# A written order for the feed-forward slots, other places for the first weight units, other engines and buffers for the output weights, and early homes in the Scan

## The chip, the cores and the metric

The kernel runs on one core of one Trainium2 chip. The metric is the device time of the whole program in microseconds (us). Of the kernel before there are three timed runs and one profiled execution, whose trace gives every time on the engines.

## The reference

The program is a trunk of two layers over 512 tokens of width 1024. Each layer is a feed-forward, a token mixer and a second feed-forward, each with a residual and a layer norm. The mixer is neighbourhood attention in the first layer and a bidirectional RWKV-7 scan in the second. The change touches the feed-forward and the end of the RWKV mixer:

```python
D_MODEL, SEQ, D_FF, DEPTH = 1024, 512, 2816, 2

def swiglu(x, w_in, w_out):
    gate, up = jnp.split(x @ w_in, 2, axis=-1)
    return (jax.nn.silu(gate) * up) @ w_out

def reference(x, ...):
    for i in range(DEPTH):
        x = layer_norm(DN_ALPHA * x + 0.5 * swiglu(x, ffn_w_in[i, 0], ffn_w_out[i, 0]), ln_g[i, 0], ln_b[i, 0])
        if i % 2 == 0:
            m = neighbourhood_attention(x, ...)
        else:
            m = rwkv7_bidir(x, ...)       # ends in ((y + bonus) * g) @ w_out
        x = layer_norm(DN_ALPHA * x + m, ln_g[i, 1], ln_b[i, 1])
        x = layer_norm(DN_ALPHA * x + 0.5 * swiglu(x, ffn_w_in[i, 1], ffn_w_out[i, 1]), ln_g[i, 2], ln_b[i, 2])
    return x
```

## The kernel before

**Precision.** Every float32 operand is held as a high and a low half (`split`, L276 to L280): ScalarE copies the raw tile to the high half (L279), VectorE subtracts it from the raw tile to get the low half (L280; another engine may be given for this second step). A product is three matmuls: high by high, high by low, low by high.

**The feed-forward** (`ffn`) runs four times. Its hidden width of 2816 is 22 column blocks f in 11 pairs c = 0 to 10. Pairs 0 to 2 (f = 0 to 5) are plain projections, whose weights `load_cols` brings into three tiles `w`. `gated` (L513) applies the silu (ScalarE, L516) and the product with the up half (VectorE, L517). From pair 3 on stands the written part, class `Seven`. There each pair is one slot: the even block is four plain products over half the depth (`plain`), the odd block is seven products of combined weights and combined tokens (`products`). The tokens' combinations are made ahead by `mixes`, parts 0 to 3. Each slot takes eleven weight units. A unit is a high and a low half in one of nine places: two halves of each of the three `w` tiles, two in `self.pair` and one in `self.one`, both ring tiles. `spots` gives out the places in turn, `weights` loads raws from memory into two raw tiles (four halves), combines them on VectorE and splits them into units.

In the written part the order of the engines' work is the order of the code. `slot` advances named generators by the words of FF_SEQ (L85): g is a piece of the plain block (the fifth g is its gated tile), s a step of the seven products, w a step of the weight generator, k a piece of the sums over the gated tile of the slot before, e the early output products of the slot before, u and z the sums over output weights (`Winograd.sums`: the first u asks for 1 MB of `w_out`, tile `ra`, L1126; the next ones make sums and splits of it; z is the third split of the pair before).

**The output part** (`Winograd`, `ffn_out`) multiplies the gated tiles by quarter blocks of `w_out`, again with combined quarters (V, t3, b22, t4). Its pieces go by c = 0, 2, 4, 6, 8, 10. The pieces c=0 and c=2 of V are opened inside the last slot, as extra steps of w (`opening`); the others by `load`, which picks the place of the raw piece and splits it. Every piece with c a multiple of four has its low half made on GpSimd, the rest on VectorE. `self.raws` is the pair of ring tiles xT that the feed-forward's input held until then.

**The Scan** (`outs`, L1932) begins the product with the RWKV output weights while the recurrence still runs. EARLY is 5: five row blocks of `w_out` are accumulated for each of eight half tiles n (four token tiles by two halves). Row blocks 0 and 1 have extra early homes, read for n = 0 and 1 (`soon`); the others are read from where they stay.

SyncE issues the DMAs of all this, in one order; ScalarE, VectorE and GpSimd each work in theirs.

Of the kernel before, what the change touches and what calls it, by code (L numbers as in the profile page):

```python
# [19 lines left out]
P = 128  # L20
D = 1024
S = 512
# [3 lines left out]
NT = S // P  # L26
# [51 lines left out]
EARLY = 5  # L78
# [3 lines left out]
DECAY = math.exp(-0.5)  # L82
GN_EPS = 64e-5
SEVEN = range(7, NF, 2)
FF_SEQ = ("g k w g w w k g w k z u g k w g s w s w s e e e s w s s u s s u s s u s e s w s e e w u")  # L85


A, B = slice(0, 64), slice(64, 128)
# [12 lines left out]
def flat2(ap):  # L101
    return ap[:, :D], ap[:, D:]


def flat(ap):
    return ap.rearrange("p a b -> p (a b)")


class Trunk:
# [28 lines left out]
    def home(self, pool):  # L138
        return self.ex or pool
# [324 lines left out]
    def ffn(self, xT, w_in, w_out, ln, nxt, lead=None):  # L464

        nc = self.nc
        npairs = NF // 2
        out = Winograd(self, w_out)
        seven = Seven(self, xT, w_in)
        with self.pool("fa") as pool:
            out.pool = pool
            keep = []
            posts = iter(())
            for c in range(npairs):
                if 2 * c + 1 in SEVEN:  # L480
                    with self.tc.manual_schedule(engines=MANUAL_SCAN):
                        raw = seven.slot(c, out, pool, posts)
                        posts = self.posts(c, raw, out, seven, keep, pool)
                        if c == npairs - 1:
                            list(posts)
                    continue
                with self.behind(*() if c or ln else (self.asked,)):
                    list(out.sums(c))
                raw = pool.tile([P, 8, 256], F32, name="ar", tag="ar", bufs=1)
                for j in range(2):  # L490
                    f = 2 * c + j
                    if f == 0:
                        pps = self.follow()
                    elif not pps:
                        us = self.units if f == 1 else [self.load_cols(w_in, FF * i + f * P, eng=nc.vector) for i in range(2)]
                        pps = [self.proj(u, pp, xT) for u, pp in zip(us, seven.banks(f))]
                    self.gated(pps.pop(0), pps.pop(0), raw[:, 3:7:3] if j else raw[:, 0:8:7])
                    if f < 4:
                        seven.mixes(f)
                    if c and j == 0:  # L500
                        list(out.early(c - 1))
                list(self.posts(c, raw, out, seven, keep, pool))
                if 2 * c + 3 in SEVEN:
                    seven.prepare()
            out.keep = {n: [k[:, n] for k in keep] for n in range(2)}
            late = npairs - 4
            out.raws = self.pair(F32)
            out.add("V", 0, out.b21, range(0, late))
            list(out.early(npairs - 1))
            out.add("V", 0, out.b21, range(late, npairs))  # L510
        return self.ffn_out(out, npairs, ln, nxt, lead)
# [403 lines left out]
class Seven:  # L915
# [57 lines left out]
    def slot(self, c, out, pool, posts):  # L973

        if 2 * c + 3 not in SEVEN:
# [3 lines left out]
                       w=self.work, k=posts, z=out.third(c - 1), u=out.sums(c, True))  # L979
        for name in FF_SEQ.split():  # L980
            next(threads[name], None)
# [12 lines left out]
    def spots(self):  # L994

        k = self.k
        two = lambda t: [h.rearrange("p (i f) -> p i f", i=2) for h in flat2(t)]
        tiles = [lambda: k.sb_w.tile([P, 2 * D], F32R, name="w", tag="w", bufs=k.nw) for _ in range(3)]
        spots = []
        for t in (tiles[0], tiles[1], lambda: self.pair, None, tiles[2]):  # L1000
            for s in two(t()) if t else [self.one]:
                spots.append(s)
                yield s
        while True:
            yield from spots

    def weights(self):
# [10 lines left out]
        def make(raw):  # L1018
            u = next(spots)
            k.split(u[:, 0], u[:, 1], raw)  # L1020
            self.units.append(u)
# [91 lines left out]
class Winograd:  # L1113
# [29 lines left out]
    def opening(self):  # L1143

        k = self.k
        raws = {}
        for c in (0, 2):
            raws[c] = k.raw()
            k.nc.sync.dma_start(raws[c].rearrange("p (c f) -> p c f", c=2), self.b21(c, 2))
            self.loads += 1  # L1150
            yield
        yield
        yield
        for c in (0, 2):
            u = k.sb_w.tile([P, 2 * D], F32R, name="w", tag="w", bufs=k.nw).rearrange("p (i f) -> p i f", i=2)
            k.split(u[:, 0], u[:, 1], raws[c])
            self.begun["b21", c] = u
            yield
# [56 lines left out]
    def load(self, src, c, lag):  # L1215
        k = self.k
        n = min(2, NF // 2 - c)
        if self.loads < 3:
            raw = k.raw()
        elif self.raws:  # L1220
            raw = self.raws[self.loads // 4 % 2][:, self.loads % 4 * D : self.loads % 4 * D + D]
        else:
            raw = self.pool.tile([P, D], F32, name="rw", tag="rw", bufs=4)
        self.loads += 1
        raw = raw[:, : n * 512]
        k.nc.sync.dma_start(raw.rearrange("p (c f) -> p c f", c=n), src(c, n))
        if lag or c == 2 and src != self.b21:
            u = self.pool.tile([P, 2, n * 512], F32R, name=f"wl{n}", tag=f"wl{n}", bufs=n)
        else:
            u = k.sb_w.tile([P, 2 * D], F32R, name="w", tag="w", bufs=k.nw)[:, : 2 * n * 512].rearrange("p (i f) -> p i f", i=2)  # L1230
        k.split(u[:, 0], u[:, 1], raw, k.nc.vector if c % 4 else k.nc.gpsimd)
        return u

    def begin(self, src):
# [153 lines left out]
class Scan:  # L1388
# [255 lines left out]
    def fetch(self, hp, z):  # L1644
        lw = self.lws[hp, z] = self.tile("lw", [P, NT, P], 2)
        self.nc.sync.dma_start(lw, self.dram["lw"][:, z, :, hp * P : (hp + 1) * P])
# [283 lines left out]
    def outs(self):  # L1930

        nc = self.nc  # L1932
        rows = lambda ap, k: ap[k * P : (k + 1) * P, :]
        home = lambda n: self.tile(n, [P, NC, 2, CH]).rearrange("p a b c -> p (a b c)")
        fetch = lambda ap, i: nc.sync.dma_start(ap, rows(self.w_out, i)).ins
        self.left = [rows(self.dram["x"], t) for t in range(NT)]
        soon = [home(n) for n in ("bk0", "ar0")]
        for i, ap in enumerate(soon):
            fetch(ap, i)
        yield  # L1940
        w = self.w = [self.az[2][:, i].rearrange("p a b -> p (a b)") for i in range(2)]
        w += [flat(self.wv)]
        fetch(w[2], 2)
        for i in range(EARLY - 1):
            nc.sync.dma_start(self.xv[:, i, :], self.dram["o"][:, i, :])
        yield
        w += [home(n) for n in ("bk1", "ar1")]
        w += [self.units[i][0].rearrange("p a b c d -> p (a b c d)") for i in (2, 4, 3)]
        for i in (3, 4, 0, 1):
            ask = fetch(w[i], i)  # L1950
        yield
        for n, (t, h) in enumerate((t, h) for t in range(NT) for h in range(2)):
            hs = slice(h * 512, (h + 1) * 512)
            x = self.tile(("e", "e2", "th")[n % 3], [P, S], 2)
            nc.sync.dma_start(x, rows(self.dram["x"], t)[:, hs])
            acc = self.k.bank("ag"[n % 2])
            for i in range(EARLY):
                u = soon[i] if n < 2 and i < 2 else w[i]
                self.wide(acc, self.xv[:, i, t * P : (t + 1) * P], u[:, hs], i == 0, i == EARLY - 1)
                if i < EARLY - 1:  # L1960
                    yield
            nc.vector.scalar_tensor_tensor(x, x, ALPHA, acc, ALU.mult, ALU.add)
            ask = nc.sync.dma_start(rows(self.dram["x"], t)[:, hs], x).ins
            if n == 0:
                with self.k.behind(ask):
                    for c in range(EARLY, ND - 1):
                        nc.sync.dma_start(w[c], rows(self.w_out, c))
            self.stored += 1
            self.reload()
            yield  # L1970
# [214 lines left out]
```

## Time and profile before

| What | us |
| --- | --- |
| timed runs, median of 3 | 2207.59 (2206.01 to 2210.19) |
| profiled execution, device time | 2204.11 |
| its span, first to last instruction | 2202.3 |
| median landing of a 256 KB raw half | 3.2 |
| median landing of the 1 MB `ra` | 8.1 |

The four feed-forwards lie in the span at about 20 to 375, 610 to 975, 975 to 1325 and 1840 to 2200 us; attention stands between the first two, the RWKV mixer between the third and the fourth. In the rows below, PE is the matmul engine, DVE is VectorE, ACT ScalarE, POOL GpSimd and SP SyncE. "PE bank L1200 <- ACT w L279" is a wait of PE at line 1200, ended by ScalarE's write of a tile `w` at line 279. Lines are those of the kernel before; in the changed kernel most lie one further on.

### The profile page before, as it was taken

The page shows a single profiled execution, that of the slowest core. Times are in us where ns is not written, and L with a number is a line of the kernel's source. Part 1 is how long each engine was busy: PE and PEld are TensorE (multiplying, and loading weights), DVE is VectorE, ACT ScalarE, POOL GpSimd, SP SyncE. Part 2 cuts the span into 40 slices and gives each one's busy share as a digit, 9 for nine tenths or more (in the row PEclk, how much of TensorE's full clock was granted, in tenths as well). Part 3 has the DMA queues.
Part 4 walks back from the last instruction along what each step waited for, and adds up shares of the span by engine and source line. Part 5 has one row for each costly group of instructions (what it writes and reads, how often), then busy time and mean ns, then how long its engine had stood idle before and what let it go on. Part 6 is the DMA issues. An engine that isn't in the chain of part 4 may idle for free.

```text
span 2202.3 us, 39167 instructions
## 1 busy us (share of the span) xinstructions
PE 2130.1 (97%) x15104; PEld 1724.3 (78%) x15104; DVE 1548.6 (70%) x2634; ACT 1087.3 (49%) x2119; POOL 513.4 (23%) x666
## 2 busy tenths in 40 slices
PE   9999989999999999899999999999999999999988
PEld 8798878888887888788888777535777558788866
DVE  7677766277486777587777669835898558677765
ACT  4354435367444454444455343636888444444434
POOL 1000025565300000340000053044788610000013
PEclk9999999999999999999999999999999999999999
DMA  6544493342243455924345754774444552544473
GB/s 190 180 158 153 154 359 121 105 126 82 96 138 130 155 171 174 361 104 155 134 155 168 263 207 144 257 240 123 119 137 130 175 188 74 167 156 163 156 282 139
DMA packets 180395, 368.39 MB, mean 167 GB/s; under 512 B 34320, under 2 KB 54416, under 8 KB 178160
## 3 DMA queue, kind: packets, MB, share of 16 engines
q1 hardware_dynamic: 180208, 365.89, 49.4%
q8 instruction: 118, 1.93, 0.4%
q14 instruction: 69, 0.57, 0.1%
HBM read 285.08 MB, written 68.68 MB: 161 GB/s over the span
## 4 chain that ended last, share of the span: by engine, by line
PE 69%; DVE 13%; DMA 11%; ACT 3%; issue 3%; POOL 0%; SPq 0%; ACTq 0%; DVEq 0%; POOLq 0%
PE bank L1200 14%; PE bank L1056 14%; PE bank L290 5%; PE bank L289 5%; PE bank L291 5%; DMA ra<-in_ffn_w_out_dram 5%; PE a L1393 5%; PE bank L352 4%; DMA raw<-in_ffn_w_out_dram 2%; DVE w L280 2%; DMA raw<-in_ffn_w_in_dram 2%; PE g L1719 2%; DVE ring L280 2%; DVE wx L280 1%; PE y L1393 1%
## 5 line engine op out<-in xcount | busy, mean ns | idle before, releaser
L280 POOL TENSOR_TENSOR w<-raw,w 128x1024 fp32r<-128x1024 f32 x34 | 83.5, 2461 | 1249.8 <-ACT w L279 1239.8
L279 ACT ACTIVATE w<-raw 128x512 fp32r<-128x512 f32 (+1 forms) x306 | 221.6, 732 | 252.9 <-DVE raw L1034 47.7
L1056 PE MATMUL bank<-xT,w 128*128 128x512 f32 (+1 forms) x1476 | 280.7, 344 | 4.5 <-ACT tmp L516 4.3
L1056 PEld LDWEIGHTS bank<-xT,w 128*128 128x128 f32 x1476 | 238.0, 189 | 43.0 <-ACT tmp L516 9.4
L280 DVE TENSOR_TENSOR w<-raw,w 128x512 fp32r<-128x512 f32 (+1 forms) x272 | 205.5, 765 | 64.0 <-ACT w L279 62.8
L1200 PE MATMUL bank<-w,ring 128*128 128x512 f32 x720 | 181.1, 409 | 29.2 <-ACT w L279 20.9
L1200 PE MATMUL bank<-wx,an 128*128 128x512 f32 x792 | 199.9, 392 | 0.0
L1200 PEld LDWEIGHTS bank<-w,ring 128*128 128x128 f32 x720 | 141.1, 198 | 66.5 <-ACT w L279 24.0
L1056 PE MATMUL bank<-xT,ring 128*128 128x512 f32 (+1 forms) x828 | 162.4, 350 | 11.6 <-ACT tmp L516 11.6
L1056 PEld LDWEIGHTS bank<-xT,ring 128*128 128x128 f32 x828 | 136.4, 190 | 34.8 <-ACT tmp L516 14.6
L1200 PEld LDWEIGHTS bank<-wx,an 128*128 128x128 f32 x792 | 142.9, 189 | 24.9
L279 ACT ACTIVATE ring<-raw 128x512 fp32r<-128x512 f32 (+1 forms) x147 | 103.5, 706 | 95.1 <-DVE raw L1034 19.1
L289 PE MATMUL bank<-xT,w 128*128 128x512 f32 x368 | 145.1, 394 | 2.5 <-DVE ar L517 2.5
L290 PE MATMUL bank<-xT,w 128*128 128x512 f32 x368 | 143.5, 390 | 0.0
L291 PE MATMUL bank<-xT,w 128*128 128x512 f32 x368 | 142.9, 390 | 0.0
L1056 PE MATMUL bank<-ring,w 128*128 128x256 f32 x1056 | 140.6, 283 | 0.0
L1056 PEld LDWEIGHTS bank<-ring,w 128*128 128x128 f32 x1056 | 135.5, 191 | 3.6
L1828 POOL TENSOR_TENSOR tm<-qs,zs 128x126 f32<-128x126 f32 (+22 forms) x248 | 107.8, 435 | 59.7 <-DVE qs L1821 22.1
L1830 POOL TENSOR_TENSOR zs<-zs,tm 128x126 f32<-128x126 f32 (+22 forms) x248 | 110.0, 444 | 19.5
L1129 DVE TENSOR_TENSOR ts<-ra 128x512 f32<-128x512 f32 x44 | 30.4, 690 | 112.5 <-DMA ra<-in_ffn_w_out_dram 101.3
L280 DVE TENSOR_TENSOR ring<-raw,ring 128x512 fp32r<-128x512 f32 (+1 forms) x123 | 85.7, 700 | 32.9 <-ACT ring L279 32.3
L280 DVE TENSOR_TENSOR wx<-ra,wx 128x512 fp32r<-128x512 f32 x132 | 89.0, 685 | 11.3 <-ACT wx L279 10.4
(383 smaller groups left out, 4600.6 us busy)
## 6 DMA issues: line engine op xcount, KB each, us to landing
raw<-in_ffn_w_in_dram SPq DMA_DIRECT2D x256, 256.0 KB, 3.2
ra<-in_ffn_w_out_dram SPq DMA_DIRECT2D x44, 1024.0 KB, 8.1
raw<-in_ffn_w_in_dram SPq DMA_DIRECT2D x48, 512.0 KB, 3.8
d_away<-away SPq DMA_DIRECT2D x44, 512.0 KB, 9.0
ring<-d_away SPq DMA_DIRECT2D x16, 1024.0 KB, 10.7
xT<-d_late SPq DMA_DIRECT2D x29, 512.0 KB, 9.6
xT<-in_ffn_w_out_dram SPq DMA_DIRECT2D x23, 512.0 KB, 9.4
d_late<-ts SPq DMA_DIRECT2D x44, 256.0 KB, 3.8
```

Source lines behind the costliest of these rows:

```text
L279: self.hi = self.nc.scalar.activation(h, raw, AF.Copy).ins
L280: self.lo = (eng or self.nc.vector).tensor_tensor(l, raw, h.bitcast(F32), ALU.subtract).ins
L289: nc.tensor.matmul(out, wh, xh, start=start, stop=False)
L290: nc.tensor.matmul(out, wh, xl, start=False, stop=False)
L291: nc.tensor.matmul(out, wl, xh, start=False, stop=stop)
L352: nc.tensor.matmul(acc[t, h], a, u[:, i, h * 512 : (h + 1) * 512], start=first and n == 0, stop=last and n == 2)
L1056: self.nc.tensor.matmul(out, w[:, i, cs], x(c)[j], start=start and c + n == 0, stop=stop and c == 3 and n == 2, skip_group_check=True)
L1200: self.nc.tensor.matmul(acc, lhs, u[:, i], start=bool(first) and m == 0, stop=last and m == 2, skip_group_check=more)
L1393: self.nc.tensor.matmul(out[hs], w[:, hs], x, start=start, stop=stop)
L1719: nc.tensor.matmul(pgs[h][:, j * P : (j + 1) * P], flat(bk[hs, q * 4 + j]), ar[hs, :, q * 4 + j], start=True, stop=True)
L1828: nc.gpsimd.tensor_tensor(tv, qs[:, s, 0:s].rearrange("p (a o) -> p a o", o=1).broadcast_to([P, s, n]), zs[:, s : s + 1, c0:].broadcast_to ...
L1830: nc.gpsimd.tensor_tensor(zs[:, 0:s, c0:], zs[:, 0:s, c0:], tv, ALU.add)
```

## The change

It has seven parts.

1. FF_SEQ is another order: "z u" moves to the slot's start, the fifth g (the gated tile of the plain block) ahead of the fifth w, and the early steps e ahead of a w.
2. The last part of the mixes is written after f = 4 rather than f = 3.
3. `spots` gives the two halves of `self.pair` and `self.one` first and the three `w` tiles after them.
4. `opening` asks for both raws in one step; the two splits come one step of w earlier.
5. `load` puts its third raw (c=4 of V) into the freed xT tile, not into one of the two raw buffers.
6. `load` makes all low halves on VectorE.
7. `outs` fetches row blocks 2 and 3 to early homes too, in halves, and reads `wv` fifth.

```diff
-FF_SEQ = ("g k w g w w k g w k z u g k w g s w s w s e e e s w s s u s s u s s u s e s w s e e w u")
+MIXED = (0, 1, 2, 4)
+FF_SEQ = ("g k z u w g w w k g w k g k g s w s w s e e e w s w s s u s s u s s u s e s w s e e w u")
...
-                    if f < 4:
-                        seven.mixes(f)
+                    if f in MIXED:
+                        seven.mixes(MIXED.index(f))
...
-        for t in (tiles[0], tiles[1], lambda: self.pair, None, tiles[2]):
+        for t in (lambda: self.pair, None, *tiles):
...
             raws[c] = k.raw()
             k.nc.sync.dma_start(raws[c].rearrange("p (c f) -> p c f", c=2), self.b21(c, 2))
             self.loads += 1
-            yield
+        yield
         yield
         yield
...
-        if self.loads < 3:
-            raw = k.raw()
-        elif self.raws:
+        if self.raws:
             raw = self.raws[self.loads // 4 % 2][:, self.loads % 4 * D : self.loads % 4 * D + D]
...
-        k.split(u[:, 0], u[:, 1], raw, k.nc.vector if c % 4 else k.nc.gpsimd)
+        k.split(u[:, 0], u[:, 1], raw)
...
-        soon = [home(n) for n in ("bk0", "ar0")]
-        for i, ap in enumerate(soon):
-            fetch(ap, i)
+        soon = {(2, h): self.tile(n, [P, S]) for h, n in enumerate(("k0", "r0"))}
+        soon.update({(3, h): flat(self.tile("lw", [P, NT, P], 2)) for h in range(2)})
+        for i, h in soon:
+            fetch(soon[i, h], i, part(h))
+        for i, n in enumerate(("bk0", "ar0")):
+            row = home(n)
+            fetch(row, i)
+            soon.update({(i, h): row[:, part(h)] for h in range(2)})
         yield
         w = self.w = [self.az[2][:, i].rearrange("p a b -> p (a b)") for i in range(2)]
+        w += [home(n) for n in ("bk1", "ar1")]
         w += [flat(self.wv)]
-        fetch(w[2], 2)
+        fetch(w[4], 4)
...
-        w += [home(n) for n in ("bk1", "ar1")]
         w += [self.units[i][0].rearrange("p a b c d -> p (a b c d)") for i in (2, 4, 3)]
-        for i in (3, 4, 0, 1):
+        for i in range(4):
             ask = fetch(w[i], i)
...
-                u = soon[i] if n < 2 and i < 2 else w[i]
-                self.wide(acc, self.xv[:, i, t * P : (t + 1) * P], u[:, hs], i == 0, i == EARLY - 1)
+                u = soon[i, n] if n < 2 and i < 4 else w[i][:, hs]
+                self.wide(acc, self.xv[:, i, t * P : (t + 1) * P], u, i == 0, i == EARLY - 1)
```

Where instructions move, the order of an engine shows it. First ScalarE (the engine of the high halves, line 279 before and 280 of the change) from the silu of the last slot of the first feed-forward into the output part. `raw` and `xT` tiles hold pieces of `w_out`, `w` their high halves. Before:

```order
L516 ACTIVATE tmp_2516<-bank_441 128x512
L1076 ACTIVATE bank_442<-bank_441 128x256
L1076 ACTIVATE tmp_2521<-bank_441 128x256
L1076 ACTIVATE tmp_2520<-bank_442 128x256
L1094 ACTIVATE tmp_2519<-bank_441 128x256
L1076 ACTIVATE tmp_2520<-bank_442 128x256
L279 ACTIVATE wx_2618<-ra_2496 128x512
L1104 ACTIVATE tmp_2519<-tmp_2520 128x256
L279 ACTIVATE w_2639<-raw_2514 128x1024
L279 ACTIVATE w_2649<-raw_2534 128x1024
L279 ACTIVATE wx_2652<-ra_2496 128x512
```

And the same place of ScalarE in the changed kernel:

```order
L517 ACTIVATE tmp_2514<-bank_441 128x512
L1077 ACTIVATE bank_442<-bank_441 128x256
L1077 ACTIVATE tmp_2519<-bank_441 128x256
L280 ACTIVATE w_2571<-raw_2532 128x1024
L1077 ACTIVATE tmp_2518<-bank_442 128x256
L1095 ACTIVATE tmp_2517<-bank_441 128x256
L1077 ACTIVATE tmp_2518<-bank_442 128x256
L280 ACTIVATE wx_2621<-ra_2458 128x512
L1105 ACTIVATE tmp_2517<-tmp_2518 128x256
L280 ACTIVATE w_2642<-raw_2534 128x1024
L280 ACTIVATE wx_2652<-ra_2458 128x512
L280 ACTIVATE w_2701<-xT_2672 128x1024
```

The piece c=0 (`w_2639`, now `w_2571`) is split five instructions earlier, in the middle of the products; c=4 (now `w_2701`, out of a part of an xT tile) follows right behind c=2 and ahead of the last `wx`, where before seven instructions stood between.

Second VectorE at the entry of the first slot of the first feed-forward. `ar` is the tile of the gated blocks, `ring_767` its kept part, `raw_774` and `raw_775` the weight generator's raw tiles, `w_780`, `w_787` and `w_818` tiles of units, `ring_260` is `self.pair` and `ring_261` `self.one`. Before:

```order
L517 SCALAR_TENSOR_TENSOR ar_619<-bank_442,tmp_678 128x2x256
L280 TENSOR_TENSOR w_780<-raw_774,w_780 128x512
L525 TENSOR_TENSOR ar_619<-ar_619 128x256
L280 TENSOR_TENSOR w_780<-raw_774,w_780 128x512
L280 TENSOR_TENSOR wx_610<-ra_601,wx_610 128x512
L280 TENSOR_TENSOR wx_613<-ra_601,wx_613 128x512
L280 TENSOR_TENSOR wx_616<-ra_601,wx_616 128x512
L280 TENSOR_TENSOR w_787<-raw_775,w_787 128x512 x2
L517 SCALAR_TENSOR_TENSOR ar_619<-bank_442,tmp_757 128x2x256
L280 TENSOR_TENSOR w_818<-raw_775,w_818 128x512
```

And in the changed kernel:

```order
L281 TENSOR_TENSOR w_789<-raw_775,w_789 128x512
L281 TENSOR_TENSOR wx_605<-ra_596,wx_605 128x512
L281 TENSOR_TENSOR wx_608<-ra_596,wx_608 128x512
L281 TENSOR_TENSOR wx_611<-ra_596,wx_611 128x512
L518 SCALAR_TENSOR_TENSOR ar_614<-bank_442,tmp_757 128x2x256
L524 TENSOR_TENSOR ar_614<-ar_614 128x256
L525 TENSOR_TENSOR ar_614<-ar_614 128x256
L281 TENSOR_TENSOR ring_767<-ar_614,ring_767 128x2x256
L527 TENSOR_TENSOR ar_614<-ar_614 128x256
L281 TENSOR_TENSOR ring_260<-raw_774,ring_260 128x512 x2
L281 TENSOR_TENSOR ring_261<-raw_775,ring_261 128x512
```

Before, four units were split between the gated tiles of f=4 (`tmp_678`) and f=5 (`tmp_757`); now only the fourth unit (`w_789`) is, and the first three, in `ring_260` and `ring_261`, stand behind the gated tile of f=5, three sums and the split of the kept part.

Third SyncE, which issues the DMAs, in the last slot of the first feed-forward. `d_late` and `d_away` are stores to memory. Before:

```order
L1016 DMA raw_774<-in_ffn_w_in_dram 128x512 x2
L1016 DMA raw_775<-in_ffn_w_in_dram 128x512 x2
L1131 DMA d_late_254<-ts_2361 128x512
L1135 DMA d_late_254<-ra_2265 128x512
L1149 DMA raw_2514<-in_ffn_w_out_dram 128x2x512
L1149 DMA raw_2534<-in_ffn_w_out_dram 128x2x512
L1126 DMA ra_2496<-in_ffn_w_out_dram 128x2x1024
L540 DMA d_away_255<-away_2510 256x1x512
L1226 DMA xT_2672<-in_ffn_w_out_dram 128x2x512
L1226 DMA xT_2672<-d_late_254 128x1024 x2
```

And in the changed kernel:

```order
L1017 DMA raw_774<-in_ffn_w_in_dram 128x512 x2
L1017 DMA raw_775<-in_ffn_w_in_dram 128x512 x2
L1132 DMA d_late_254<-ts_2361 128x512
L1136 DMA d_late_254<-ra_2222 128x512
L1127 DMA ra_2458<-in_ffn_w_out_dram 128x2x1024
L1150 DMA raw_2532<-in_ffn_w_out_dram 128x2x512
L1150 DMA raw_2534<-in_ffn_w_out_dram 128x2x512
L541 DMA d_away_255<-away_2510 256x1x512
L1225 DMA xT_2672<-in_ffn_w_out_dram 128x2x512 x2
L1225 DMA xT_2672<-d_late_254 128x1024
```

The 1 MB load `ra` now stands ahead of the two opening loads, and two pieces go into the xT tile in a row, one of them c=4; before, c=4 was asked for into `raw_2700` eleven instructions further on.

More of the change, by code (lines that the diff above doesn't have):

```diff
@@ L1934, in outs @@
         home = lambda n: self.tile(n, [P, NC, 2, CH]).rearrange("p a b c -> p (a b c)")
-        fetch = lambda ap, i: nc.sync.dma_start(ap, rows(self.w_out, i)).ins
+        part = lambda h: slice(h * 512, (h + 1) * 512)
+        fetch = lambda ap, i, cs=slice(None): nc.sync.dma_start(ap, rows(self.w_out, i)[:, cs]).ins
         self.left = [rows(self.dram["x"], t) for t in range(NT)]
-        soon = [home(n) for n in ("bk0", "ar0")]
-        for i, ap in enumerate(soon):
-            fetch(ap, i)
+        soon = {(2, h): self.tile(n, [P, S]) for h, n in enumerate(("k0", "r0"))}
[6 more added lines that the diff above has]
+            soon.update({(i, h): row[:, part(h)] for h in range(2)})
         yield
         w = self.w = [self.az[2][:, i].rearrange("p a b -> p (a b)") for i in range(2)]
+        w += [home(n) for n in ("bk1", "ar1")]
         w += [flat(self.wv)]
-        fetch(w[2], 2)
+        fetch(w[4], 4)
         for i in range(EARLY - 1):
```

## The prediction

> **What bounds the kernel now.** The page comes first, with the busy shares; then the waits of the matmul engine (each row: what waited, for what, us in total, times, longest).
>
> ```profile
> span 2202.3 us, 39167 instructions
> PE 2130.1 (97%) x15104; PEld 1724.3 (78%) x15104; DVE 1548.6 (70%) x2634; ACT 1087.3 (49%) x2119; POOL 513.4 (23%) x666
> ```
>
> ```profile
> PE bank L1200 <- ACT w L279: 20.9, 5, 5.7
> PE bank L1056 <- ACT tmp L516: 15.8, 14, 3.1
> PE bank L1200 <- POOL w L280: 5.4, 4, 1.7
> PE bank L1200 <- DVE w L280: 2.8, 4, 0.8
> PE a L1393 <- DMA wv<-in_rw_out_dram: 2.4, 1, 2.4
> ```
>
> PE is busy for 97% of the span, and the change removes no matmul. So only the time in which PE stands still, or runs at a lower clock, can be won. Three places matter: L1200, where each feed-forward enters its output part (20.9 + 5.4 + 2.8 = 29.1 us, four times); L1056, the slots of the written part, behind the silu of L516 (15.8 us); one row of the Scan (2.4 us).
>
> **The ends.** The timeline of PE, SyncE, ScalarE, GpSimd and VectorE at the end of the first feed-forward (start, us, engine, line, count, idle time before):
>
> ```profile
> 280.89 0.45 SPq L1226 DMA_DIRECT2D xT<-in_ffn_w_out_dram  x1
> 294.99 5.55 PE L1200 MATMUL bank<-w,ring 128*128 128x512 f32 x23 [0.76 <-DVE w L280]
> 298.35 0.38 SPq L1226 DMA_DIRECT2D raw<-in_ffn_w_out_dram  x1
> 308.57 1.06 ACT L279 ACTIVATE w<-raw 128x1024 fp32r<-128x1024 f32 x1 [0.23 <-DMA raw<-in_ffn_w_out_dram]
> 309.68 1.22 PE L1200 MATMUL bank<-w,ring 128*128 128x512 f32 x2 [5.07 <-ACT w L279]
> 309.71 2.37 POOL L280 TENSOR_TENSOR w<-raw,w 128x1024 fp32r<-128x1024 f32 x1 [285.82 <-ACT w L279]
> 312.13 13.78 PE L1200 MATMUL bank<-w,ring 128*128 128x512 f32 x52 [1.23 <-POOL w L280]
> 328.47 12.40 PE L1200 MATMUL bank<-w,ring 128*128 128x512 f32 x54
> ```
>
> Weight piece c=4 waits for one of the two raw buffers that c=0 and c=2 hold, is asked for at 298.35, lands about 10.2 us later, and is split by ScalarE, then in 2.37 us by GpSimd. PE loses 0.76 + 5.07 + 1.23 = 7.06 us. It then runs slowly: the windows (start:end, length, busy time of PE, PEld, DVE, ACT, POOL, then granted clock, DMA share, GB/s) show a clock of 0.61.
>
> ```profile
> 312.10:316.00 3.90, 3.87 (x11) 3.11 (x12) 3.90 (x2) 0.00 (x0) 3.31 (x1) 0.61 0.96 349
> 312.10:365.00 52.90, 52.87 (x233) 43.59 (x234) 30.67 (x36) 24.09 (x29) 28.48 (x12) 0.97 0.46 175
> 293.71 1.23 DVE L280 TENSOR_TENSOR w<-raw,w 128x1024 fp32r<-128x1024 f32 x1 [0.53 <-ACT w L279]
> ```
>
> ```profile
> 907.19 14.56 PE L1200 MATMUL bank<-w,ring 128*128 128x512 f32 x52 [1.72 <-POOL w L280]
> 1269.55 14.29 PE L1200 MATMUL bank<-w,ring 128*128 128x512 f32 x52 [1.23 <-POOL w L280]
> 2135.94 14.72 PE L1200 MATMUL bank<-w,ring 128*128 128x512 f32 x52 [1.22 <-POOL w L280]
> ```
>
> At the pace of 328.47 (12.40 us for 54) 52 matmuls take 11.94 us. The four stretches took 13.78, 14.56, 14.29 and 14.72: 9.6 us too long in all. An end thus costs (29.1 + 9.6) / 4 = 9.7 us.
>
> After the change c=4 needs no raw buffer: it goes into a freed xT tile, which is free once the first product of the last slot has read it: the row at 280.89 is the load into that tile before, 17.5 us ahead of 298.35. c=0 and c=2 are split inside the slot. Even with the 10.2 us again, c=4 is there by 291, its high half (the tile for it comes free at about 292) by 294 and its low half (1.23 us on VectorE) by about 296; PE wants it at 296.3 (294.99 plus six matmuls). The next pieces come likewise 2 to 3 us ahead of need. I take the whole 38.7 us as gone. From the other side, if c=4 or the early sums behind it are late by about 3 us, 12 us stay.
>
> The cost: VectorE takes 11 low halves per feed-forward from GpSimd, 11 x 1.23 = 13.5 us. The row 312.10:365.00 has VectorE busy 30.67 of 52.90 us, so it fits beside 52.87 us of matmuls, which hide it; with that cover gone it would cost up to 4 x 13.5 = 54 us. I count nothing. The two opening loads keep their place in the queue to within a step, and the mix written one block later comes out at the same place in every engine's order: nothing either.
>
> **The slots.** A regular slot of the first feed-forward starts at 216.36:
>
> ```profile
> 216.36 8.32 PE L1056 MATMUL bank<-xT,w 128*128 128x512 f32 x36
> 223.25 3.56 SPq L1016 DMA_DIRECT2D raw<-in_ffn_w_in_dram  x4
> 227.17 0.57 ACT L516 ACTIVATE tmp<-bank 128x512 f32<-128x512 f32 x1
> 227.68 0.38 SPq L1126 DMA_DIRECT2D ra<-in_ffn_w_out_dram  x1
> 227.80 1.69 PE L1056 MATMUL bank<-xT,ring 128*128 128x256 f32 x12 [0.39 <-ACT tmp L516]
> 232.84 1.59 PE L1056 MATMUL bank<-ring,w 128*128 128x256 f32 x12
> 236.42 0.69 DVE L1129 TENSOR_TENSOR ts<-ra 128x512 f32<-128x512 f32 x1 [3.54 <-DMA ra<-in_ffn_w_out_dram]
> ```
>
> The products wait for the silu (227.17), which stands behind splits on ScalarE. With the gated tile ahead of them it is done some 2 us before the products, and with "z u" at the slot's start the 1 MB `ra` is asked 9 us earlier, so VectorE's 3.54 us go as well (PE did not wait for those). VectorE's four sums of `ra` and ScalarE's `wx` splits move with it, into time in which PE runs the plain block out of units that are ready. The first slot of each feed-forward has the larger waits; the rows show three, and the groups behind two of them:
>
> ```profile
> 87.81 11.04 PE L1056 MATMUL bank<-xT,w 128*128 128x512 f32 x48
> 88.01 0.69 DVE L517 SCALAR_TENSOR_TENSOR ar<-bank,tmp 128x512 f32<-128x512 f32 x1 [3.00 <-PE bank L291]
> 89.29 0.42 DVE L523 TENSOR_TENSOR ar<-ar 128x256 f32<-128x256 f32 x1
> 101.58 1.69 PE L1056 MATMUL bank<-xT,ring 128*128 128x256 f32 x12 [2.73 <-ACT tmp L516]
> 697.00 2.59 PE L1056 MATMUL bank<-xT,ring 128*128 128x256 f32 x12 [2.92 <-ACT tmp L516]
> 699.39 2.24 PE L1056 MATMUL bank<-ring 128*128 128x256 f32 x12
> 1057.76 1.77 PE L1056 MATMUL bank<-xT,ring 128*128 128x256 f32 x12 [3.07 <-ACT tmp L516]
> 1059.33 2.76 PE L1056 MATMUL bank<-ring 128*128 128x256 f32 x12
> ```
>
> These three are 8.7 of the 15.8 us. I count all 15.8 as gone, and set against them a new wait in the first three feed-forwards. There the first unit's split now stands on VectorE behind the gated tile of f=5, which can't start before 88.01: 0.69, three small sums (0.42 alone as at 89.29, some 0.35 when one follows another), the kept tile's split and its own (0.69 each, the shape of the row at 236.42) make it ready near 91.1. PE's first two matmuls need only high halves; its third wants the low one at 88.27. That is 2.9 us, and the later reload of the raw buffers pushes the silu about 0.5 us behind the first products: 3.4 us, three times, +10.2. Its bounds are 0 (the splits get ahead) and 3 x 5 us (behind a late raw as well). In the fourth the first units are split earlier.
>
> **The clock** is a term of its own. Waits of 2.92 and 3.07 us were followed by slow groups: 2.59 + 2.24 us instead of twice 1.60, and 2.76 instead of 1.60 with some more behind it, 1.6 us each. Behind 2.73 us the group took 1.69, so nothing was lost. The new waits of 2.9 us lie between these cases; I take two of three as tripping again, which cancels the 3.3 us won. Bounds: 3.3 us better to 1.6 worse. The Trainium skill, "TensorE: Matmul & The Clock Gate", Part 1, says that a free-running window of about 3.4 us watches PE, and that one idle window halves the clock. This trace disagrees on the idle time, since less than 3.1 us tripped it. By the page's rule no first-slot wait would slow PE, before or after, and the sum would stay where it is or be some 3 us better.
>
> **The Scan.** PE waits for weight row `wv`, third in the order:
>
> ```profile
> 1730.15 1.03 PE L1393 MATMUL a<-ar,xraw 128*64 128x512 f32 x4
> 1733.54 1.08 PE L1393 MATMUL a<-wv,xraw 128*64 128x512 f32 x4 [2.36 <-DMA wv<-in_rw_out_dram]
> 1734.96 1.89 PE L1393 MATMUL a<-bk,xraw 128*64 128x512 f32 x4
> 1737.06 1.75 PE L1393 MATMUL a<-ar,xraw 128*64 128x512 f32 x4
> ```
>
> The two groups behind it took 1.89 and 1.75 instead of 1.03, 1.6 us more. Rows 2 and 3 now come from early homes and `wv` is fifth, two rows later, when it has landed: -2.4 - 1.6 = -4.0. The four half rows asked for in addition (1 MB) go out ahead of the stretch, while the Scan's recurrence keeps PE, with no wait on a DMA in the rows of waits other than this one. At worst they push `wv` back by as much as it gained, and nothing is won.
>
> **Sum against the profiled execution** (span 2202.3 us, 2204.11 with what lies around it): -38.7 - 15.8 + 10.2 + 0 - 4.0 = -48.3 us. That execution lies 3.5 us under the median of 2207.59, so the forecast is 2207.6 - 48.3 = **2159 us**. About 0.2%, 4.4 us, is what a measurement of this kernel can tell from no change.
>
> **Rivals.**
> - *The ends win half.* Everything about c=4 to c=8 rests on DMA latency while the queues are full (0.96 in the row 312.10). If the new order only moves the wait to another piece, about 3 us and a slow clock stretch stay per end: 4 x (3 + 1.5) = 18 us, 2177. For it: margins of 0.5 to 3 us. Against: c=4's DMA has 17 us more. 0.2.
> - *No new first-slot wait*, because the engines' queues resolve sooner than I walked: 3 x 3.4 less, 2149. Against: the written order puts f=5 ahead. 0.08.
> - *All three new waits trip the clock* and last 5 us: +5 +1.6 = 2166. 0.08. It lies inside the range.
> - *Slower.* With `ra` at the slot's start, each slot's weight raws queue behind 1 MB. They are asked from 223.25; the third product starts at 232.84, 9.6 us later, of which two splits take 1.3, so a raw later than 8.3 us stalls PE. `ra` itself took 227.68 to 236.42, 8.7 us, but is asked 4.5 us ahead of the raws then. Per us beyond 8.3 it costs 28 slots x 1 us; from 8.3 + 48.3/28 = 10.0 us on the kernel is slower than before, and at 11 us it gives 2159 + 28 x 2.7 = 2235. 0.04.
> - *The change doesn't do what it says* in the first slots is in the forecast already; at the ends it would need c=4 to wait on something other than the buffer. About 2200 then, 0.02.
>
> **The numbers.** Forecast 0.58, the others as given. The range: 2148 (no new wait, less 1) to 2181 (the half-won ends, plus the Scan's 4), which leaves out the slower cases and a part of the tails. Faster 0.94, within 0.2% 0.02, slower 0.04.
>
> **What would show it.** Right: the waits of L1201 on ScalarE and GpSimd are gone, GpSimd has no split in the ends, the granted clock there is 1.00, and the silu waits of the slots are near 0; three waits of about 3 us on VectorE's first unit appear at the first slots; `wv` is waited for no more. Wrong: a wait at L1201 for another `w` or for `an`, products waiting for a raw's DMA, or VectorE above 90% in the ends with PE waiting for its splits.

## The result and the profile after

| | median, us | runs |
| --- | --- | --- |
| before | 2206.80 | 2205.91 to 2210.19 (4) |
| changed | 2156.41 | 2155.64 to 2157.19 (4) |

The ratio is 0.9769, with a 95% interval of 0.9752 to 0.9786: 50.4 us less, where 48.3 were forecast from the profiled execution. The two profiled executions stand at 2204.11 and 2155.64 us, 48.5 apart. In two later sets of runs the changed kernel came out at 2157.89 (ratio 0.9806, 0.9791 to 0.9821) and 2157.09 (0.9803, 0.9785 to 0.982). The changed kernel hardly moved, the kernel before did: its medians there were 2200.7 and 2199.0, so the gain was 43 and 42 us in those sets. The size of the gain depends on the chip and the set by some 8 us.

The profile page of the changed kernel, first part, and then three rows picked from the waits of PE:

```profile
span 2153.8 us, 39197 instructions
PE 2120.4 (98%) x15104; PEld 1716.8 (80%) x15104; DVE 1574.5 (73%) x2678; ACT 1080.5 (50%) x2119; POOL 403.9 (19%) x622
```

```profile
PE bank L1057 <- ACT ring L280: 6.1, 3, 2.0
PE bank L1057 <- DVE ring L281: 1.6, 3, 0.5
PE bank L1057 <- ACT tmp L517: 0.3, 1, 0.3
```

The same number of matmuls has 9.7 us less busy time: that is clock, granted at 0.988 of full speed on average before and at 0.996 now. The waits at the output part (29.1 us before, L1201 now) and on `wv` have left the list, the silu has 0.3 us left of 15.8. New are 6.1 + 1.6 = 7.7 us in three first slots.

The end of the first feed-forward in the changed kernel, by its timeline, with two windows behind it. The first is the whole stretch; the second begins where PE reaches c=4, as 312.10:365.00 did in the kernel before:

```profile
282.87 1.30 SPq L1225 DMA_DIRECT2D xT<-in_ffn_w_out_dram  x2
294.49 1.04 ACT L280 ACTIVATE w<-xT 128x1024 fp32r<-128x1024 f32 x1
295.45 8.32 PE L1201 MATMUL bank<-w,ring 128*128 128x512 f32 x36
296.17 1.22 DVE L281 TENSOR_TENSOR w<-xT,w 128x1024 fp32r<-128x1024 f32 x1
```

```profile
290.00:342.60 52.60, 52.60 (x247) 44.09 (x246) 38.61 (x54) 25.43 (x30) 0.00 (x0) 1.00 0.86 338
301.00:353.90 52.90, 52.90 (x235) 43.80 (x234) 39.14 (x59) 25.66 (x31) 0.72 (x1) 1.00 0.64 254
```

c=4 is asked for at 282.87 and its low half is done at 297.4. PE runs 36 matmuls without a gap, at full clock, and from c=4 on VectorE is busy for 39.14 us of 52.90 in place of 30.67. The pieces c=0 and c=2 hold four column blocks with six matmuls each, so PE has 24 matmuls ahead of the first of c=4 and wants that piece near 295.45 + 24 x 0.23 = 301.

The entry to the first slot, in the first feed-forward, then PE's rows at the same place of the second and third, and the clock window of the first:

```profile
87.48 0.39 PE L292 MATMUL bank<-xT,w 128*128 128x512 f32 x1
88.70 0.63 ACT L280 ACTIVATE ring<-ar 128x512 fp32r<-128x512 f32 x1 [5.64 <-DVE ar L518]
89.24 1.66 ACT L280 ACTIVATE ring<-raw 128x512 fp32r<-128x512 f32 x3
89.90 0.78 PE L1057 MATMUL bank<-xT,ring 128*128 128x512 f32 x2 [2.03 <-ACT ring L280]
90.44 1.89 DVE L281 TENSOR_TENSOR ring<-raw,ring 128x512 fp32r<-128x512 f32 x3
91.18 9.26 PE L1057 MATMUL bank<-xT,ring 128*128 128x512 f32 x34 [0.50 <-DVE ring L281]
104.84 1.36 PE L1057 MATMUL bank<-ring,w 128*128 128x256 f32 x10
```

```profile
677.96 9.39 PE L1057 MATMUL bank<-xT,ring 128*128 128x512 f32 x34 [0.54 <-DVE ring L281]
691.61 1.60 PE L1057 MATMUL bank<-ring,w 128*128 128x256 f32 x12
1029.64 9.34 PE L1057 MATMUL bank<-xT,ring 128*128 128x512 f32 x34 [0.54 <-DVE ring L281]
```

```profile
90.45:93.85 3.40, 2.90 (x7) 2.15 (x7) 3.35 (x6) 1.70 (x3) 0.00 (x0) 0.50 0.44 142
```

ScalarE had been idle for 5.64 us before the kept tile's split at 88.70, and the first unit's split stands behind that. PE waits 2.03 + 0.5 us, and then runs at half clock for 3.4 us. From the last matmul of f=5 (87.48) to the slot's second product (104.84) it is 17.4 us. Most of the wait is for ScalarE's high half; VectorE's low half, which the prediction had in mind, adds the 0.5 us.

### The profile page after: what moved, and what is told of

It is laid out like the page before. It is cut to its first block, busy times and chain, and to the rows that moved or that the text cites. A ratio compares the mean times of both kernels' runs of the same rounds, so it can differ in the third digit from the quotient of the medians.

```text
span 2153.8 us, 39197 instructions
## 1 busy us (share of the span) xinstructions
PE 2120.4 (98%) x15104; PEld 1716.8 (80%) x15104; DVE 1574.5 (73%) x2678; ACT 1080.5 (50%) x2119; POOL 403.9 (19%) x622
## 4 chain that ended last, share of the span: by engine, by line
PE 79%; DVE 11%; ACT 6%; issue 2%; DMA 0%; ACTq 0%; DVEq 0%; SPq 0%
PE bank L1057 19%; PE bank L1201 17%; PE bank L291 6%; PE bank L290 6%; PE bank L292 6%; PE a L1392 5%; PE bank L353 4%; DVE wx L281 2%; PE g L1718 2%; DVE w L281 1%; PE y L1392 1%; ACT ring L280 1%; DVE ring L281 1%; ACT w L280 1%; PE bank L1585 1%
## 5 line engine op out<-in xcount | busy, mean ns | idle before, releaser
L280 ACT ACTIVATE w<-raw 128x512 fp32r<-128x512 f32 (+1 forms) x302 | 214.9, 727 | 237.7 <-DVE raw L1036 56.3
L1057 PE MATMUL bank<-xT,w 128*128 128x512 f32 (+1 forms) x1572 | 303.6, 347 | 1.4 <-ACT tmp L517 0.3
L1057 PEld LDWEIGHTS bank<-xT,w 128*128 128x128 f32 x1572 | 254.5, 189 | 47.3 <-ACT tmp L517 10.9
L447 POOL COPY marks<-x 128x1 f32<-128x1 f32 x8 | 8.2, 1028 | 1054.5 <-DVE x L439 1053.0
L1201 PE MATMUL bank<-wx,an 128*128 128x512 f32 x792 | 200.8, 392 | 0.0
L1201 PE MATMUL bank<-w,ring 128*128 128x512 f32 x720 | 169.1, 390 | 0.0
L1201 PEld LDWEIGHTS bank<-wx,an 128*128 128x128 f32 x792 | 142.5, 189 | 24.9
L1201 PEld LDWEIGHTS bank<-w,ring 128*128 128x128 f32 x720 | 135.0, 188 | 28.9 <-DVE w L281 0.2
L1057 PE MATMUL bank<-xT,ring 128*128 128x512 f32 (+1 forms) x732 | 146.1, 352 | 8.2 <-ACT ring L280 6.1
L1057 PEld LDWEIGHTS bank<-xT,ring 128*128 128x128 f32 x732 | 120.4, 193 | 31.3 <-ACT ring L280 7.4
L1057 PE MATMUL bank<-ring,w 128*128 128x256 f32 x960 | 127.8, 283 | 0.0
L1057 PEld LDWEIGHTS bank<-ring,w 128*128 128x128 f32 x960 | 123.2, 191 | 3.3
L281 POOL TENSOR_TENSOR w<-raw,w 128x1024 fp32r<-128x1024 f32 x30 | 74.0, 2475 | 85.6 <-ACT w L280 79.6
## 6 DMA issues: line engine op xcount, KB each, us to landing
ring<-d_away SPq DMA_DIRECT2D x16, 1024.0 KB, 10.2
```

What stands on the lines that cost most here:

```text
L280: self.hi = self.nc.scalar.activation(h, raw, AF.Copy).ins
L281: self.lo = (eng or self.nc.vector).tensor_tensor(l, raw, h.bitcast(F32), ALU.subtract).ins
L1057: self.nc.tensor.matmul(out, w[:, i, cs], x(c)[j], start=start and c + n == 0, stop=stop and c == 3 and n == 2, skip_group_check=True)
L1201: self.nc.tensor.matmul(acc, lhs, u[:, i], start=bool(first) and m == 0, stop=last and m == 2, skip_group_check=more)
```

## The experiments

All times are medians of four runs or more, each set on one chip. The changed kernel was in the second and third set (2157.89 and 2157.09). It was not in the first, which is read against 2156 to 2158. No run undoes part 2 of the change (the place of the last mix) alone, or the three moves within FF_SEQ one by one.

### First set: one part undone, and one edit more

**undo_xt**, c=4 in a raw buffer again:

```diff
-        if self.raws:
+        if self.loads < 3:
+            raw = k.raw()
+        elif self.raws:
```

> The changed kernel with one part undone: the third output piece (c=4) is again loaded into a raw buffer. Theory A (the ends are won because c=4 no longer waits for that buffer): the load can go out only after c=0's split, near 287 us on the changed kernel's timeline, lands 10 to 13 us later, is split by about 303 us and PE wants it after the early sums, near 303 to 305: waits of 0 to 3 us at each of the four ends, up to a slow-clock stretch each, in all 5 to 20 us more than the changed kernel, 2162 to 2176. Theory B (splitting c=0 earlier and the low halves on VectorE won the ends, the buffer is beside the point): 2156 within 3 us. Theory C (the buffer is all of it): 38.7 us come back, 2195.

It took 2162.6 us, some 5 to 6 more than the changed kernel: theory A at its low end. Its end of the first feed-forward:

```profile
288.00 0.45 SPq L1227 DMA_DIRECT2D raw<-in_ffn_w_out_dram  x1
301.46 1.06 ACT L280 ACTIVATE w<-raw 128x1024 fp32r<-128x1024 f32 x1 [1.39 <-DMA raw<-in_ffn_w_out_dram]
305.25 9.23 PE L1201 MATMUL bank<-w,ring 128*128 128x512 f32 x40
```

The load leaves at 288, right behind c=0's early split, and takes 13 us. It still arrives in time, since PE does the early output products before it. Only 3.0 us of waits on `w` came back in all four ends.

**undo_seq**, the old FF_SEQ:

```diff
-FF_SEQ = ("g k z u w g w w k g w k g k g s w s w s e e e w s w s s u s s u s s u s e s w s e e w u")
+FF_SEQ = ("g k w g w w k g w k z u g k w g s w s w s e e e s w s s u s s u s s u s e s w s e e w u")
```

> The changed kernel with the old order FF_SEQ. Theory A (the order won the slots): the regular slots' silu waits come back (5.9 us in sum: 15.8 less the three first slots' 8.7 and the fourth's 1.3, plus that 1.3), and in the first slots the silu wait is added to the new wait for the first unit (up to 3 us each): 2163 to 2172, and VectorE waits for the 1 MB load again. Theory B (the slots were won by the places of the units): within 2 us of 2156.

2180.17 us, 22 to 24 more: theory A, and past its range. The waits of PE show where the rest is:

```profile
PE bank L1057 <- ACT tmp L517: 13.1, 9, 3.9
PE bank L1201 <- DVE w L281: 7.7, 6, 2.3
PE bank L1057 <- ACT ring L280: 6.1, 3, 2.0
```

The silu waits are back (13.1 us) on top of the new first-slot waits, with 7.7 us at the ends, which the theory had not counted, and more slow clock (0.993 granted in place of 0.996).

**undo_places**, the old order of places:

```diff
-        for t in (lambda: self.pair, None, *tiles):
+        for t in (tiles[0], tiles[1], lambda: self.pair, None, tiles[2]):
```

> The changed kernel with the old order of places for the units (two w tiles first). Theory A (the new wait in the first slots, 2.54 us in three feed-forwards, comes from the new places, since in the written-out order the units in the w tiles stand ahead of the gated tile of f=5 and those in the ring places behind it): these three waits and the slow clock behind each (34 matmuls in 9.26 us instead of 7.8, 1.4 us) go: 3 x 3.9 = 12 us less than the changed kernel, 2145; the silu wait of the first slots stays away, since the new order puts the gated tile ahead. Theory B (the old places bring the first slots' silu wait of 2.7 to 3.1 us back): 2155 to 2160. Theory C (the places matter at the ends, where w tiles must be free for c=0 and c=2): waits at the ends, over 2160.

2142.76 us: theory A, and **faster than the changed kernel**. The first two units are split at 73.19 us, where the changed kernel splits its first at 89.24, and the 48 matmuls run through:

```profile
73.19 1.16 ACT L280 ACTIVATE w<-raw 128x512 fp32r<-128x512 f32 x2 [2.94 <-issue]
87.90 11.04 PE L1057 MATMUL bank<-xT,w 128*128 128x512 f32 x48
```

No wait of over 0.25 us is left at L1057 or at L1201.

**early_units**, the new places, with the first units prepared ahead of the gated tile of f=5:

```diff
+                    if j and 2 * c + 3 in SEVEN:
+                        seven.prepare()
                     self.gated(pps.pop(0), pps.pop(0), raw[:, 3:7:3] if j else raw[:, 0:8:7])
...
-                if 2 * c + 3 in SEVEN:
-                    seven.prepare()
```

> The changed kernel with one more edit: the first units are prepared ahead of the gated tile of f=5 in the code, not behind the pair's sums. Their splits then stand ahead of it on ScalarE and VectorE, which were idle there for 5.6 and 9.6 us. Theory A (the first-slot wait is queue order and nothing else): the three waits and their slow-clock stretches go, 3 x 3.9 = 12 us, 2145, and the granted clock has no slow stretch in the feed-forwards. Theory B (the raws or the places come no earlier): no change, 2156. Theory C (earlier splits push back the gated tile of f=5 and its sums): a new wait of 1 to 3 us in the first slots, 2150 to 2160.

2144.02 us: theory A again. The first unit now goes into its ring place at 68.45 us, and PE reads the ring units without a wait:

```profile
68.45 0.63 ACT L280 ACTIVATE ring<-raw 128x512 fp32r<-128x512 f32 x1 [0.15 <-DMA raw<-in_ffn_w_in_dram]
87.83 8.32 PE L1057 MATMUL bank<-xT,ring 128*128 128x512 f32 x36
```

So the new places can be kept and the wait avoided, but nothing shows that the places then win anything over the old ones.

### Second set: what won the ends

**changed_again** is the changed kernel, unedited.

> The changed kernel itself, beside the others on one chip, as their reference: 2156 by its own earlier runs, with three first-slot waits of 2.0 + 0.5 us. If this chip is the quicker one of the last runs, up to 0.3% less.

2157.89 us, with the three first-slot waits as before.

**old_with_xt** is the kernel before with only c=4 in the xT tile.

```diff
-        if self.loads < 3:
-            raw = k.raw()
-        elif self.raws:
+        if self.raws:
```

> The kernel before with one part of the change: c=4 goes into the freed xT tile. Theory A (the wait for the raw buffer is the ends' loss): c=4's split then stands right behind c=2's on ScalarE, and the waits of 4.4 to 5.7 us with the slow clock behind them go; 0.5 to 0.8 us for c=0 stays, and GpSimd's low half of 2.4 us may leave up to 1 us: 2207 - 38.7 + 4 x (0.8 to 1.8) = 2171 to 2176. Theory B (the buffer is worth what undoing it cost, 6 us, and the rest came with the other parts): 2195 to 2203.

2166.68 us against 2200.66 in that set (ratio 0.9846, 0.983 to 0.9862), 34 us from one part: theory A. (Its range was counted from 2207; as a gain it is 31 to 36 us, and 34 lies in it.) The end of its first feed-forward:

```profile
290.34 1.99 ACT L279 ACTIVATE w<-raw 128x1024 fp32r<-128x1024 f32 x2
292.69 8.72 PE L1200 MATMUL bank<-w,ring 128*128 128x512 f32 x37 [0.46 <-DVE w L280]
292.76 1.05 ACT L279 ACTIVATE w<-xT 128x1024 fp32r<-128x1024 f32 x1
293.88 2.49 POOL L280 TENSOR_TENSOR w<-xT,w 128x1024 fp32r<-128x1024 f32 x1 [269.97 <-ACT w L279]
```

c=0 and c=2 are as late as ever and GpSimd takes 2.49 us for c=4's low half, yet only 0.46 us of waiting is left here, 2.8 us in the four ends.

**undo_open**, the changed kernel with the old steps of the opening:

```diff
             self.loads += 1
+            yield
-        yield
```

> The changed kernel with the old opening: one raw asked in each step, the splits of c=0 and c=2 one step later, behind the last product's silu copies. Theory A: as before, PE waits 0.5 to 0.8 us for c=0's low half at each end and for nothing more, since c=4 has its own tile: +2 to +4 us. Theory B (the early split of c=0 is what won the ends): waits of several us return, +10 us or more.

2158.95 us, 1.1 more than the changed kernel. That is less than A expected, and the two sets of runs overlap. No wait at the ends is over 0.25 us.

**undo_xt_open** has both edits, of undo_xt and undo_open.

> The changed kernel with both undone: c=4 in a raw buffer, and the old opening. Theory A (early opening and own tile are two cures of one wait: c=4's load leaves when a raw buffer is free or needs none): alone each undoing costs little, together the end wait comes back: c=4 asked for near 295 us, landed near 305 to 308, 3 to 6 us of waiting at each end and 2 us of slow clock: +20 to +30 us, 2176 to 2186. Theory B (they add): the sum of the two single undoings, +8 to +10 us.

2198.87 us, 41 more than the changed kernel, where the single undoings cost 5 and 1. This is theory A in kind; B is out, and the size is past A's range. Its end of the first feed-forward, with VectorE's rows:

```profile
298.76 0.38 SPq L1227 DMA_DIRECT2D raw<-in_ffn_w_out_dram  x1
307.81 1.06 ACT L280 ACTIVATE w<-raw 128x1024 fp32r<-128x1024 f32 x1 [0.21 <-DMA raw<-in_ffn_w_out_dram]
308.92 1.22 PE L1201 MATMUL bank<-w,ring 128*128 128x512 f32 x2 [3.68 <-ACT w L280]
304.60 5.47 DVE L555 SCALAR_TENSOR_TENSOR x<-x,bank 128x512 f32<-128x512 f32 x9 [2.58 <-PE bank L1201]
309.99 1.22 DVE L281 TENSOR_TENSOR wl<-xT,wl 128x1024 fp32r<-128x1024 f32 x1
311.12 1.87 DVE L555 SCALAR_TENSOR_TENSOR x<-x,bank 128x512 f32<-128x512 f32 x3
312.92 1.22 DVE L281 TENSOR_TENSOR w<-raw,w 128x1024 fp32r<-128x1024 f32 x1
314.19 14.14 PE L1201 MATMUL bank<-w,ring 128*128 128x512 f32 x52 [4.05 <-DVE w L281]
```

The load leaves at 298.76, as late as in the kernel before (298.35). And once the piece is late, its low half on VectorE is later than it was on GpSimd: it stands behind twelve residual sums (L555) and another split, and is done at 314.1, 5 us after the high half. PE waits 4.05 us for it, where it waited 1.23 for GpSimd. Over the four ends PE waits 11.4 us for high halves and 20.5 us for low ones.

### Third set: the Scan, VectorE, and the places once more

**changed_third** is the changed kernel, unedited.

> The changed kernel once more, as the reference for the other three on one chip: 2156 to 2158.

2157.09 us.

**undo_scan** has `outs` of the kernel before:

```diff
-        soon = {(2, h): self.tile(n, [P, S]) for h, n in enumerate(("k0", "r0"))}
...
+        soon = [home(n) for n in ("bk0", "ar0")]
...
-        fetch(w[4], 4)
+        fetch(w[2], 2)
...
-                u = soon[i, n] if n < 2 and i < 4 else w[i][:, hs]
+                u = soon[i] if n < 2 and i < 2 else w[i]
```

> The changed kernel with the old homes and order of rows in the Scan. Theory A (the prediction's term): PE waits for wv again, 2.4 us and up to 1.6 us of slow clock, +4 us, 2160 to 2162; a second wait for the next row (the run of the old kernel with c=4 in the xT tile had 1.5 + 2.3 us) would make it +4 to +6. Theory B (the wait was an accident of where the stretch fell): within 1.5 us.

2160.62 us, 3.5 more: theory A. The two sets of four runs do not overlap. In its Scan PE waits for `wv` and, two rows later, for another thing:

```profile
1708.35 1.08 PE L1392 MATMUL a<-wv,xraw 128*64 128x512 f32 x4 [1.72 <-DMA wv<-in_rw_out_dram]
...
1711.82 1.08 PE L1392 MATMUL a<-ar,xraw 128*64 128x512 f32 x4 [0.74 <-DVE vt L1907]
```

This run also shows when the clock falls. At the first slot of the second feed-forward the same wait of 2.04 + 0.54 us did not lower it. Behind the rows stand two windows, the first of this run's first slot, where the clock fell, the second of this one:

```profile
678.01 0.73 PE L1057 MATMUL bank<-xT,ring 128*128 128x512 f32 x2 [2.04 <-ACT ring L280]
679.29 8.00 PE L1057 MATMUL bank<-xT,ring 128*128 128x512 f32 x34 [0.54 <-DVE ring L281]
...
691.28 1.70 PE L1057 MATMUL bank<-xT,w 128*128 128x256 f32 x12 [1.27 <-ACT tmp L517]
692.82 1.36 PE L1057 MATMUL bank<-ring,w 128*128 128x256 f32 x10
```

```profile
90.10:93.50 3.40, 3.34 (x7) 2.25 (x8) 3.40 (x7) 2.21 (x4) 0.00 (x0) 0.50 0.29 99
677.20:680.60 3.40, 2.05 (x8) 1.39 (x9) 3.37 (x8) 3.06 (x6) 0.00 (x0) 1.00 0.08 18
```

The 34 matmuls take 8.00 us instead of 9.39, but then PE waits 1.27 us for the silu, which in the changed kernel's run came in time. From the first of the 34 to the second product it is 13.5 us (679.29 to 692.82) here and 13.7 (677.96 to 691.61) there: this slot costs the same either way.

**undo_dve**, the low halves of c = 0, 4 and 8 on GpSimd:

```diff
-        k.split(u[:, 0], u[:, 1], raw)
+        k.split(u[:, 0], u[:, 1], raw, k.nc.vector if c % 4 else k.nc.gpsimd)
```

> The changed kernel with the low halves of c = 0, 4 and 8 on GpSimd again (2.4 us each instead of 1.2). Theory A (with its load early, a low half has more slack than that): no wait of PE on GpSimd at the ends, or under 0.5 us each, within 2 us of the changed kernel. Theory B (the 5.4 us that PE waited for GpSimd before return): waits of 1 to 2 us at each end and slow clock behind some, +5 to +10 us.

2156.39 us, 0.7 less than the changed kernel, within what the runs can tell: theory A, and PE waits for no split of GpSimd's. Nor does this part give VectorE more busy time: it was busy for 1580.1 us here, and for 1574.5 us in the changed kernel, which has 44 VectorE instructions more. In this run splits on VectorE took up to 3.44 us beside one on GpSimd, where the same shape takes 1.22 us alone:

```profile
318.68 3.10 POOL L281 TENSOR_TENSOR w<-xT,w 128x1024 fp32r<-128x1024 f32 x1 [1.03 <-ACT w L280]
319.42 3.44 DVE L281 TENSOR_TENSOR w<-xT,w 128x1024 fp32r<-128x1024 f32 x1
```

**undo_places_2** is undo_places again, beside the changed kernel.

> The changed kernel with the old places again, beside the changed kernel on one chip: no first-slot waits and no slow-clock stretch outside the program's end; three waits of 2.57 us and three stretches of 3.4 us at half clock (1.4 us each) gone: 12 us less than the changed kernel. A rival with the places worth half of that (the chip of the earlier run was quicker): 6 us.

2143.14 us, 14.0 less than the changed kernel on the same chip; against the kernel before 0.9737 (0.9723 to 0.9752). There is no first-slot wait and no slow stretch behind one:

```profile
87.67 0.39 PE L292 MATMUL bank<-xT,w 128*128 128x512 f32 x1
87.89 11.04 PE L1057 MATMUL bank<-xT,w 128*128 128x512 f32 x48
100.21 1.60 PE L1057 MATMUL bank<-ring 128*128 128x256 f32 x12
```

From the last matmul of f=5 to the second product it is 12.5 us, 4.8 less than in the changed kernel. Three times that is 14.5 us, close to the 14.0 of the two medians.

## Why the prediction was right, and where it was off

**The ends** (-38.7 us): right in size, and in the main cause. The four end waits and the slow clock are gone, and c=4's tile alone brought 34 us to the kernel before. Two steps were off. The prediction let PE want c=4 at 296.3, "294.99 plus six matmuls"; 24 matmuls come first and it is 301, so the slack is 3.5 us and not a few tenths. There was luck in this: the low half was done at 297.4, which by the prediction's own time would have been some 1 us late at each end. And the prediction saw in the new opening only an earlier split of c=0 and c=2, and counted the rest as "nothing". It is a second cure of the wait for c=4: undoing the tile alone costs 5 us, undoing the opening alone 1, undoing both 41. Either makes c=4's load leave 10 us or more earlier. The opening alone in the kernel before was not run.

**VectorE for GpSimd** (0): right, and the load was smaller than it took. The prediction gave VectorE 4 x 13.5 = 54 us more to do, covered by matmuls. VectorE's busy time rose by 25.9 us from the kernel before, and undo_dve, where this part alone is undone, has no less of it than the changed kernel. The cover holds, since the piece is early. With a late piece the low half stands behind the residual sums, and that is part of the 41 us.

**The slots** (-15.8 + 10.2): the silu's 15.8 us went to 0.3. The new wait was there, in the three feed-forwards named, of the size forecast: the third matmul starts at 91.18 us, where 87.48 + 3 x 0.23 = 88.2 would be its time, 3.0 us late (forecast 2.9; the view of waits shows 2.03 + 0.5, since the two early matmuls lie between). VectorE's first split was done at 91.1, as forecast. What the prediction left out is ScalarE: the first unit's high half stood there behind the kept tile's split, and so behind the gated tile of f=5, and PE waited 2.03 of the 2.5 us for it. The "0.5 us" of silu behind it is not to be seen as a wait where the clock was lowered.

**The clock in the slots** (0): all three waits tripped it, not two of three, but each stretch cost 9.26 to 9.39 us instead of 8.00, 1.3 to 1.4 us where 1.65 was taken. 4.0 us against the 3.3 of before makes +0.7. That the term came out near 0 is in part luck: more trips than forecast, each of them cheaper. The prediction took the slow clock and the late silu as two terms; in undo_scan they take each other's place. In all, the three first slots cost 14.0 us by the medians; the prediction's terms had 10.2 + 3.3 = 13.5.

**The Scan** (-4.0): undoing it cost 3.5 us. The two executions split it differently: 2.4 us and a slow clock in one, 1.72 + 0.74 us of waits in the other. The last 1 us of the 3.5 is not told apart.

**The sum** of these terms by the two profiles is -38.7 - 15.5 + 7.7 + 0.7 - 4.0 = -49.8 us; 48.5 were measured between them. That counts the new first slots by their waits and slow stretches (11.7 us); by their length they cost some 14, which makes -47.5. The rest of some 1 us stays open. The sum fits the chip from whose trace it was worked out; in the later sets, where the kernel before was quicker, the whole change won 42 to 43 us. The order FF_SEQ is worth more than its 15.8 us: without it the changed kernel also waits at the ends.

So the change is the sum of a large gain and one part that takes back 14 us. The new places are free early, as early_units shows; it is the order of the splits, written behind the gated tile of f=5, that is late. The best kernel of the study is the change without its new places, 2142.8 and 2143.1 us.

## What to carry to other kernels

When a load waits for a buffer, there can be two cures, another buffer or an earlier release; test them singly and together, since each alone can hide what the other is worth. A free place for data is no gain if the work that fills it is queued behind something late: read the order on each engine, not the list of buffers. And before counting a piece as late, find the matmul that really wants it.

## What the runs showed of the hardware

A wait far below 3.4 us halved the clock: 2.03 us did, three times, and 2.36 us in the Scan before, while 2.73 us in the first slot before did not, nor the 2.04 us of undo_scan. The slow stretches of the changed kernel begin at 90.45, 677.55 and 1029.12 us, which are 172.0 and 103.0 steps of 3.413 us apart. Laid out in such steps, the waits fall differently:

| wait of PE | step ends at | idle in the step before, and in the one behind | clock behind it |
| --- | --- | --- | --- |
| changed, 87.87 to 89.90 | 90.45 | 2.03, 0.50 | 0.50 |
| before, Scan, 1731.18 to 1733.54 | 1731.7 and 1735.1 | 0.5, then 1.9 | 0.50 from 1735.1 |
| before, first slot, 98.85 to 101.58 | 100.1 | 1.25, 1.48 | 1.00 |
| undo_scan, 675.97 to 678.01 | 677.2 | 1.23, 0.81 + 0.54 | 1.00 |

The steps of undo_scan are counted from its slow stretch at 90.10, those of the kernel before from the one at 1735.1. This fits the free-running window of the Trainium skill ("TensorE: Matmul & The Clock Gate", Part 1), which lets the clock fall after a whole idle window of about 3.4 us. Here less was enough: about 1.9 us of idle time within one step lowered the clock, and 1.5 us did not. Two waits that left 1.5 us or less in either step passed. This reading fits these waits, but no run set out to shift one.

A split on VectorE was slower beside a split on GpSimd. In undo_dve the eleven splits `w<-xT` of 128x1024 on VectorE took 2.28 us on average and up to 3.44. In the changed kernel, where GpSimd makes none at the ends, the forty of this kind took 1.22. Why, no run here shows.
